# Neighbourhood attention: the products with the values of three query tiles issued in one stretch

## The chip, the core and the metric

The kernel runs on one core of a Trainium2 chip. Its engines work side by side, each through its own queue of instructions in a fixed order: PE (TensorE, matmuls; PEld is the part of it that loads weights), DVE (VectorE), ACT (ScalarE), POOL (GpSimd) and SP (here it issues transfers). SBUF is the on-chip working memory of 128 partitions; PSUM, in eight banks, is where PE writes its results. The metric is the device time of one execution in microseconds (us); less is better. All numbers in this part come from the runs and from one profiled execution of the kernel before.

## The reference

Two layers of a diffusion backbone are computed on 1024 latent tokens (a grid of 16 rows by 64 columns) and 128 context tokens, with a model width of 1024. The first layer has mLSTM heads and grouped-query attention; the change does not touch it. The second layer is neighbourhood attention with 16 heads of width 64: each latent token attends to a window of 8 rows by 16 columns around it and to all 128 context keys, in one softmax. Cut to what matters:

```
s_loc = q_r . k_win * scale + bias              # the window's keys
s_ctx = q_r . kc * scale                        # the 128 context keys
p = softmax(concat([s_loc, s_ctx]))
o = p_loc . v_win + p_ctx . vc
y = (o * silu(z)) @ w_out
```

The last products of `p` with the values `v` and `vc` are what the change moves.

## The kernel before

The kernel is written in a framework that traces the Python code, then orders each engine's instructions by a list scheduler with a model of their times, and inserts the waits. So the order on PE is not the order of the code: while one piece waits for its input, the scheduler puts ready work of another piece ahead of it. A block under `manual_schedule` for an engine keeps its own order there, as one piece.

The second layer (the phase named "na", function `run`, L1383 to L1422) handles the 16 heads as eight pairs, `p` = 0 to 7. For a pair, `na_proj` computes queries, keys, values and the gate from the layer's input. These projections are products in three parts (L328 to L330, and L343 to L345 with the operands swapped), because each number is split into a high and a low part. `na_pair` (L1172) then walks over the queries: eight tiles of 128 latent tokens and one tile of context tokens, in three groups `c` of three tiles. A tile of 128 tokens covers all 16 grid rows of eight neighbouring columns, so its window lies in at most three tiles of keys; with the context keys these are `nk` = 3 (first and last tile) or 4 blocks of 128 keys. The projections of pair p+1 are traced while pair p's attention is under way, and the scheduler mixes both on PE. The last pair has no successor; pieces of its own projections (`late`) and the first tiles of the output projection (`out`) stand in for it.

`na_unit` (L1195) does one tile for both heads of the pair:

- scores (L1210): two products for each head into a bank `s`;
- softmax for each head: DVE adds the bias and finds the maximum (L1216), ACT takes the exponential and the sum (L1218), DVE the reciprocal (L1219), POOL the scaling (L1220), all in a piece of the ring `sb`;
- turning (L1223, recorded at L106): PE transposes the `nk` blocks of weights into the one bank `tr` (in the last pair, the second head uses `ptr`); ACT and DVE take turns to copy that bank into a piece of the ring `pt` (L101, L103);
- products with values (L1227 to L1231): `nk` blocks, and for each block head 0 and then head 1, accumulate in the bank `o`. A product has 64 output rows; the two heads use the two halves of PE's columns (`tile_position=(0, b)`), so their results land in the two halves of `o`.

The three tiles of a group share a bank `o`, of which there is one. Behind the group, `put_y` (L969) multiplies it by the gate into `y` and sends it to memory for the output projection. The ninth tile (context queries) goes through `ctx_unit` (L1004), whose two products with values stand at L1001. All eight pairs together hold 480 products at L1231 (60 in a pair: 6 + 6 x 8 + 6) and 16 at L1001.

The ring `pt` has four pieces of 512 columns, two in each of two tiles (L1390); a piece is free again when the products that read it are done.

Of the kernel before, what the change touches and what calls it, by code (L numbers as in the profile page):

```python
# [18 lines left out]
P = 128  # L19
# [7 lines left out]
DHB = 64  # L27
# [12 lines left out]
class Kern:  # L40
# [42 lines left out]
    def smg(self, w):  # L83
        return self.sp.tile([P, 4], F32, tag="smg", bufs=16, name=self.name("smg"))[:, :w]

    def ring(self, n, bufs):

        ts = [self.u([P, 2, 512], n=n) for _ in range(bufs // 2)]
        turn = itertools.cycle([t[:, i] for t in ts for i in range(2)])
        return lambda: next(turn)  # L90

    def const(self, shape, n, dt=F32):
# [1079 lines left out]
    def na_pair(self, p, terms, v, gz, vc):  # L1172

        nc, a = self.nc, self.a
        bias = []
        for hh in range(2):
            b = self.u([P, T], n="bias")
            nc.sync.dma_start(b, a["na_bias"][2 * p + hh])
            bias.append(b)
        y = self.ytile()  # L1180
        for c in range(NC):
            po = self.ps("o")
            for t in range(3):
                if t:
                    yield y
                j = 3 * c + t
                o = po[:, t * P : (t + 1) * P]
                if j < 8:
                    self.na_unit(terms, v, vc, bias, j, o, p == 7)
                else:  # L1190
                    self.ctx_unit([terms(hh, 8, 11, 1) for hh in range(2)], [v[:, 8, 0:DHB], v[:, 8, DHB:]], o, self.pt)
            self.put_y(p, slice(c * CW, (c + 1) * CW), po, gz, y)
            yield y

    def na_unit(self, terms, v, vc, bias, j, po, alone):  # L1195

        nc = self.nc
        j0, j1 = max(j - 1, 0), min(j + 1, 7)

        k0 = j0 + j0 // 3 + (j0 % 3 > 0)  # L1200
        at = int(k0 % 4 > 0)
        nk = j1 - j0 + 2
        n = nk * P

        first, step, w = (2, 1, P) if j == 0 else (2, 3, P) if j == 7 else (1, 5, 256) if at else (0, 6, 256)
        grid = lambda t: t.rearrange("p (a k) -> p a k", k=w)
        pts, ss = [], [self.ps("s") for _ in range(2)]
        for hh in range(2):
            for part, (x, y) in enumerate(terms(hh, j, k0, nk)):
                nc.tensor.matmul(ss[hh][:, :n], x, y, start=part == 0, stop=part == 1)  # L1210
        for hh in range(2):
            x = self.sb()[:, :n]
            nm = self.sm(1)
            b = bias[hh]
            b = bass.AP(b.tensor, b.offset + first * P, [list(b.ap[0]), [step * P, n // w], [1, w]])
            nc.vector.tensor_tensor_reduce(grid(x), grid(ss[hh][:, :n]), b, -1.0, -NEG, ALU.add, ALU.min, nm)  # L1216
            r = self.sm(1)
            nc.scalar.activation(x, x, AF.Exp, bias=nm, scale=-1.0, accum_out=r)  # L1218
            nc.vector.reciprocal(r, r)  # L1219
            nc.gpsimd.tensor_scalar(x, x, r, 1.0, ALU.mult, ALU.mult)  # L1220
            tr = self.ps("ptr" if alone and hh else "tr")
            for i in range(nk):
                self.flipped(tr[:, i * P : (i + 1) * P], x[:, i * P : (i + 1) * P])  # L1223
            pt = self.pt()
            self.evac(pt[:, :n], tr[:, :n])
            pts.append(pt)
        for i in range(nk):  # L1227
            for hh in range(2):
                b = hh * DHB
                vs = vc[:, b : b + DHB] if i == at else v[:, j0 + i - (i > at), b : b + DHB]  # L1230
                nc.tensor.matmul(po[b : b + DHB, :], vs, pts[hh][:, i * P : (i + 1) * P], start=i == 0, stop=i == nk - 1, tile_position=(0, b))  # L1231


    def run(self):
        nc, a = self.nc, self.a
# [80 lines left out]
        with self.phase("mlstm", ("e", 3, [P, 4, CW])):  # L1316
            self.ts = [self.decays_load(0, g) for g in range(NC)]
            start = self.mlstm_start(0)
# [3 lines left out]
            for hd in range(HA):  # L1322
# [3 lines left out]
                if hd < HA - 1:  # L1326
                    pr = nxt
                    blocks(hd + 1, evs, (2, 3, 4))
                    start = self.mlstm_start(hd + 1)
# [12 lines left out]
        with self.phase("gqa"):  # L1342
            self.pt = self.ring("pt", 14)
            ahead = (w.append(self.w_out(0, k)) for k in range(KB))
            with self.tc.manual_schedule(engines={mybir.EngineType.PE}):
                last = self.gqa(Q, gz, early, ahead)
        gg = [self.load_gg(0, 0, self.raw())]
        h = []
        with self.phase("out0"):
            new = lambda: self.t("x", 5, [P, D])  # L1350
            ys = [self.load_y(i, last) for i in range(2)]
            for c in range(NC):
# [16 lines left out]
                for i in tiles:  # L1369
# [7 lines left out]
                    o, ss = (new(), self.sm(2)) if c < 2 else os[i % 3]  # L1377
# [5 lines left out]
        with self.phase("na"):  # L1383
            self.klo = [self.t(f"kl{j}", 1, [P, 12, P], F32R) for j in range(2)]
            for hh in range(2):
                nc.gpsimd.memset(self.klo[hh][DHB - hh * DHB : 2 * DHB - hh * DHB].bitcast(F32), 0.0)
            for p in range(8):
                tiles, late = self.na_proj(h, p, first)
                if p == 0:
                    self.sb, self.pt = (self.ring(n, 4) for n in ("sb", "pt"))  # L1390
                unit = self.na_pair(p, *tiles)
                if p < 7:
                    for j, _ in enumerate(unit):
                        if late and j in (1, 4, 7):
                            late.pop(0)()
            w, ys, gg = [], [], []

            def out(i):
                if i in (0, 6):
                    gg.append(self.load_gg(1, i // 6, self.u([P, D], n="gg")))  # L1400
                if i + 1 < NT:
                    ys.append(self.load_y(i + 1, last))
                xt = self.u([P, D], n="x")
                nc.sync.dma_start(xt, self.x1d[i * P : (i + 1) * P, :])
                o, ss = self.u([P, D], n="o"), self.sm(2)
                for n in range(2):
                    self.out_half(ys[i], w, n, o, ss, gg[i // 8])
                self.out_end(o, ss, xt, a["out_ys"][i * P : (i + 1) * P, :] if i < 8 else a["out_yp"], 1 + i // 8)

            for j, last in enumerate(unit):  # L1410
                for f in late[j : j + 1]:
                    f()
                for k in range(3 * j, min(3 * j + 3, KB)):
                    w.append(self.w_out(1, k))
                if j == 0:
                    ys = [self.load_y(0, last, False)]
                if j == 2:
                    self.late_y()
                if j in (4, 6):
                    out(j // 2 - 2)  # L1420
            for i in range(2, NT):
                out(i)  # L1422
# [137 lines left out]
```

## Time and profile before

| | |
|---|---|
| median of 3 runs | 1607.9 us (1607.58 to 1609.25) |
| the profiled execution: its time | 1609.35 us |
| its span, first to last instruction | 1607.5 us |
| PE busy | 1555.3 us, 97% of the span |
| DVE / ACT / POOL busy | 848.7 / 655.7 / 603.4 us |
| mean granted TensorE clock | 0.994 |
| records of products with values at L1231 | 960, from 914.7 to 1532.9 us |

The table is of the page that the profiler's data were condensed to. "Busy" is the time in which an engine had an instruction under way. A matmul's end is modelled, and matmuls overlap: a PE that is busy all the time may still lose time between two of them. What a matmul costs is therefore read from the spacing of starts, not from durations. A product of full fp32 numbers, as the turnings' and the values' are, shows as passes: the 480 products at L1231 are 960 records, two for each.

In rows of a timeline, a row is: start in us, duration in us (of the whole row when several equal instructions are merged), engine, line, operation, output<-inputs, rows*columns of the weights and partitions x elements of what is streamed, count, and in brackets the engine's idle time before it with what ended it.

### The profile page before, as it was taken

What the parts mean: (1) busy time and instruction counts of PE and PEld (TensorE: products, weight loads), DVE (VectorE), ACT (ScalarE), POOL (GpSimd) and SP (SyncE); (2) the same over time, 40 slices, a digit from 0 to 9 for tenths busy, and PEclk for the clock granted to TensorE, in tenths of its full rate; (3) what the DMA queues carried; (4) which work ended last, traced back from release to release, by engine and by line L of the source; (5) the groups of instructions that cost most, each with busy time, mean ns of one, the idle gap of its engine ahead of it and who ended that gap; (6) DMA issues with size and microseconds to landing.
All of it is one profiled execution on the core that took longest, in us unless ns stands there. A gap on an engine that the chain in (4) does not pass through costs nothing.

```text
span 1607.5 us, 27178 instructions
## 1 busy us (share of the span) xinstructions
PE 1555.3 (97%) x10190; PEld 1392.0 (87%) x10190; DVE 848.7 (53%) x2324; ACT 655.7 (41%) x1568; POOL 603.4 (38%) x820
## 2 busy tenths in 40 slices
PE   6999998999999899999999999999999999999998
PEld 4899898999999787777889899989998999878776
DVE  3533897974558666774555433343434343446432
ACT  2622212122245677875444433343434333346321
POOL 2415645554446545663224222332323232334100
PEclk9999999999999999999999999999999999999999
DMA  9103635422310000221332212130303030316332
GB/s 358 50 27 108 229 124 193 160 83 90 113 53 28 16 30 22 69 75 62 126 127 97 63 50 83 34 99 22 99 19 99 23 99 19 95 42 193 99 127 79
DMA packets 73122, 143.81 MB, mean 89 GB/s; under 512 B 15466, under 2 KB 44446, under 8 KB 72990
## 3 DMA queue, kind: packets, MB, share of 16 engines
q1 hardware_dynamic: 68692, 127.05, 23.8%
q10 hardware_dynamic: 4298, 15.02, 2.4%
q8 instruction: 81, 1.33, 0.3%
q14 instruction: 51, 0.42, 0.1%
HBM read 115.47 MB, written 21.86 MB: 85 GB/s over the span
## 4 chain that ended last, share of the span: by engine, by line
PE 85%; DVE 8%; ACT 3%; issue 2%; DMA 1%; POOL 1%; SPq 0%; DVEq 0%; POOLq 0%; ACTq 0%
PE pj L330 12%; PE pj L328 12%; PE pj L329 11%; PE pj L343 7%; PE pj L345 7%; PE pj L344 7%; PE tr L106 5%; PE o L1231 5%; PE s L1210 4%; PE o L910 3%; PE s L870 3%; DVE mj L248 3%; PE ptr L106 2%; PE pj L106 2%; DVE pr L871 1%
## 5 line engine op out<-in xcount | busy, mean ns | idle before, releaser
L328 PE MATMUL pj<-hh,whi 128*128 128x384 f32 x1176 | 402.0, 342 | 1.2 <-ACT qT L101 0.5
L330 PE MATMUL pj<-hh,wlo 128*128 128x384 f32 x1176 | 399.5, 341 | 0.6 <-POOL wlo L115 0.6
L329 PE MATMUL pj<-hl,whi 128*128 128x384 f32 x1176 | 399.8, 340 | 0.0
L328 PEld LDWEIGHTS pj<-hh,whi 128*128 128x128 f32 x1176 | 221.6, 188 | 4.4 <-issue 0.7
L329 PEld LDWEIGHTS pj<-hl,whi 128*128 128x128 f32 x1176 | 221.7, 188 | 2.5 <-issue 0.9
L330 PEld LDWEIGHTS pj<-hh,wlo 128*128 128x128 f32 x1176 | 221.3, 188 | 2.6 <-POOL wlo L115 0.8
L1220 POOL TENSOR_SCALAR sb<-sb,sm 128x512 f32<-128x512 f32 (+1 forms) x128 | 85.8, 672 | 306.5 <-DVE sm L1219 289.7
L115 POOL TENSOR_TENSOR wlo<-raw,whi 128x1024 fp32r<-128x1024 f32 x59 | 143.5, 2433 | 133.8 <-ACT whi L114 79.1
L880 POOL TENSOR_SCALAR pr<-pr,smg 128x384 f32<-128x384 f32 x192 | 114.3, 615 | 83.4 <-DVE smg L878 57.1
L1218 ACT ACTIVATE sb<-sb,sm 128x512 f32<-128x512 f32 (+1 forms) x128 | 89.0, 696 | 90.8 <-DVE sm L1216 87.0
L343 PE MATMUL pj<-whi,hh 128*128 128x256 f32 x432 | 122.7, 284 | 1.0 <-DVE v L1136 0.8
L344 PE MATMUL pj<-wlo,hh 128*128 128x256 f32 x432 | 122.1, 283 | 0.0
L345 PE MATMUL pj<-whi,hl 128*128 128x256 f32 x432 | 122.0, 283 | 0.0
L248 DVE CUSTOM_DVE_ANT_0 mj<-wm,cb 128x512 f32<-128x512 f32 x128 | 114.0, 891 | 3.8 <-DMA wm<-in_w_modT_dram 1.8
L871 DVE CUSTOM_DVE_ANT_0 pr<-s,zero 128x384 f32<-128x384 f32 x192 | 102.3, 553 | 24.1 <-PE s L870 23.1
L343 PE MATMUL pj<-whi,yh 128*128 128x512 f32 x288 | 114.1, 396 | 0.0
L344 PE MATMUL pj<-wlo,yh 128*128 128x512 f32 x288 | 114.0, 396 | 0.0
L345 PE MATMUL pj<-whi,yl 128*128 128x512 f32 x288 | 113.6, 395 | 0.0
L870 PE MATMUL s<-Kst,Q 128*128 128x384 f32 x384 | 105.4, 370 | 4.6 <-DVE smg L871 3.7
L1216 DVE CUSTOM_DVE_ANT_1 sb<-s,bias 128x512 f32<-128x512 f32 (+1 forms) x112 | 74.6, 666 | 52.9 <-PE tr L106 49.7
L114 ACT CAST whi<-raw 128x1024 fp32r<-128x1024 f32 x76 | 79.2, 1044 | 29.3 <-DMA raw<-in_w_out_dram 8.3
L343 PEld LDWEIGHTS pj<-whi,hh 128*128 128x128 f32 x432 | 81.4, 188 | 2.9 <-DVE v L1136 1.2
(344 smaller groups left out, 3035.1 us busy)
## 6 DMA issues: line engine op xcount, KB each, us to landing
wm<-in_w_modT_dram SPq DMA_DIRECT2D x32, 512.0 KB, 4.4
raw<-in_w_c_dram SPq DMA_DIRECT2D x25, 512.0 KB, 3.5
raw<-in_w_ab_dram SPq DMA_DIRECT2D x24, 512.0 KB, 4.4
e<-rbd ACTq DMA_DIRECT2D x12, 768.0 KB, 6.1
bias<-in_na_bias_dram SPq DMA_DIRECT2D x16, 576.0 KB, 4.1
wm<-in_w_mod_dram SPq DMA_DIRECT2D x16, 512.0 KB, 6.9
raw<-in_w_out_dram SPq DMA_DIRECT2D x16, 512.0 KB, 3.7
y<-yd SPq DMA_DIRECT2D x18, 448.0 KB, 3.5
```

The costliest lines, as they stand in the source:

```text
L106: self.nc.tensor.transpose(out, in_, self.ident)
L115: (eng_lo or nc.gpsimd).tensor_tensor(lo, src, hi.bitcast(F32), ALU.subtract)
L248: nc.vector.tensor_tensor_reduce(junk, w[:, b, :], cb[:, r, :], 1.0, 0.0, ALU.mult, ALU.add, mp[:, hf, q // 4, 2 * (q % 4) + b, r : r + 1])
L328: nc.tensor.matmul(ps[:, :CW], a, hh, start=k == 0, stop=False)
L329: nc.tensor.matmul(ps[:, :CW], a, hl, start=False, stop=False)
L330: nc.tensor.matmul(ps[:, :CW], b, hh, start=False, stop=k == KB - 1)
L343: nc.tensor.matmul(ps[:, :width], hh, a, start=k == 0, stop=False)
L344: nc.tensor.matmul(ps[:, :width], hh, b, start=False, stop=False)
L345: nc.tensor.matmul(ps[:, :width], hl, a, start=False, stop=k == KB - 1)
L870: nc.tensor.matmul(s[:, :CW], x, y, start=part == 0, stop=part == 1)
L871: nc.vector.tensor_tensor_reduce(pr[:, c, :], s[:, :CW], zero, -1.0, -NEG, ALU.add, ALU.min, m3[:, c : c + 1])
L880: nc.gpsimd.tensor_scalar(pr[:, c, :], pr[:, c, :], r, 1.0, ALU.mult, ALU.mult)
```

## The change

`na_unit` no longer issues the products with values. It returns a function `values` that will, and `na_pair` collects these for the tiles of a group and calls them together behind the group's last tile, in a block that keeps its order on PE. The tiles are taken from the last to the first; inside a tile, head 1 goes ahead of head 0. Since the turned weights of three tiles now have to be kept, the ring `pt` gets seven pieces instead of four: the three new ones are tiles of the phase's own pool (one of two pieces, one of one).

```
-    def ring(self, n, bufs):
+    def ring(self, n, bufs, more=()):
-        ts = [self.u([P, 2, 512], n=n) for _ in range(bufs // 2)]
-        turn = itertools.cycle([t[:, i] for t in ts for i in range(2)])
+        ts = [self.u([P, 2, 512], n=n) for _ in range(bufs // 2)] + list(more)
+        turn = itertools.cycle([t[:, i] for t in ts for i in range(t.shape[1])])
...
             po = self.ps("o")
+            last = []
             for t in range(3):
...
-                    self.na_unit(terms, v, vc, bias, j, o, p == 7)
+                    last.append(self.na_unit(terms, v, vc, bias, j, o, p == 7))
...
+            with self.tc.manual_schedule(engines={mybir.EngineType.PE}):
+                for f in last[::-1]:
+                    f()
             self.put_y(p, slice(c * CW, (c + 1) * CW), po, gz, y)
...
-        for i in range(nk):
-            for hh in range(2):
-                b = hh * DHB
...
+        def values():
+            for i in range(nk):
+                for hh in (1, 0):
+                    b = hh * DHB
...
+        return values
...
-                    self.sb, self.pt = (self.ring(n, 4) for n in ("sb", "pt"))
+                    self.sb, self.pt = self.ring("sb", 4), self.ring("pt", 4, [self.t(f"pt{j}", 1, [P, 2 - j, 512]) for j in range(2)])
```

No instruction is added or taken away on any engine. What moves on PE is seen best in the first group of the first pair. Before, on PE (`s` scores, `tr` turned weights of a tile's head, `o<-pt` products with values, where `vc` are the context's values and `v` the latent tokens'; the number behind a name tells buffers apart):

```order
L106 MATMUL tr_9800<-cc,sb_9778 128x128 x3
L1210 MATMUL s_9860<-k_1670_9381,q_9379 128x512
L1210 MATMUL s_9860<-kl_1662_9369,q_9379 128x512
L1231 MATMUL o_9787<-pt_9780,vc_9373 64x128
L1210 MATMUL s_9861<-k_1671_9382,q_9380 128x512
L1210 MATMUL s_9861<-kl_1663_9370,q_9380 128x512
L106 MATMUL tr_9811<-cc,sb_9778 128x128 x3
L106 MATMUL ptr_9773<-cc,kp_9383 128x128
L1210 MATMUL s_9901<-k_1670_9381,q_9379 128x512
L1210 MATMUL s_9901<-kl_1662_9369,q_9379 128x512
L1231 MATMUL o_9787<-pt_9780,vc_9373 64x128
L1231 MATMUL o_9787<-pt_9780,v_9378 64x128 x4
```

One product of head 0, ready as soon as that head is turned, stands alone between scores; the tile's other five follow once head 1 is turned. With the change the products of this group, on PE:

```order
L1215 MATMUL s_10026<-k_1670_9381,q_9379 128x512
L1215 MATMUL s_10026<-kl_1662_9369,q_9379 128x512
L1238 MATMUL o_9789<-pt_1706_9780,v_9378 64x128 x2
L1238 MATMUL o_9789<-pt_1706_9780,vc_9373 64x128 x2
L1238 MATMUL o_9789<-pt_1706_9780,v_9378 64x128 x4
L1238 MATMUL o_9789<-pt_9783,vc_9373 64x128 x2
L1238 MATMUL o_9789<-pt_9783,v_9378 64x128 x6
L1238 MATMUL o_9789<-pt_9782,vc_9373 64x128 x2
L1238 MATMUL o_9789<-pt_9782,v_9378 64x128 x4
L106 MATMUL tr_9918<-cc,sb_9779 128x128 x4
```

All 22 products of three tiles stand in a row, two heads by turns, the third tile's first. Counted over all of the second layer, with the context tile's pairs of L1001: before, 133 unbroken runs of such products (61 of one product, 8 of two, 15 of five, 1 of six, 46 of seven, 2 of eight); with the change 24 runs (in each pair one of 22, one of 24, one of 16, of which two are the context tile's).

The other place is in pair 6, fourth and fifth tile, where no projection is at hand that could stand between the pieces. Before, on PE:

```order
L106 MATMUL tr_14548<-cc,sb_9779 128x128 x4
L106 MATMUL tr_14560<-cc,sb_9779 128x128 x4
L1231 MATMUL o_14535<-pt_9781,v_13208 64x128
L1210 MATMUL s_14654<-k_2389_14204,q_14202 128x512
L1210 MATMUL s_14654<-kl_1663_9370,q_14202 128x512
L1210 MATMUL s_14691<-k_2388_14203,q_14201 128x384
L1210 MATMUL s_14691<-kl_1662_9369,q_14201 128x384
L1231 MATMUL o_14535<-pt_9781,v_13208 64x128
L1231 MATMUL o_14535<-pt_9781,vc_14103 64x128 x2
L1231 MATMUL o_14535<-pt_9781,v_13208 64x128 x4
L106 MATMUL tr_14586<-cc,sb_9778 128x128 x4
L106 MATMUL tr_14598<-cc,sb_9778 128x128 x4
```

With the change, the same part between two stretches of products, on PE:

```order
L106 MATMUL tr_14607<-cc,sb_9779 128x128 x4
L106 MATMUL tr_14619<-cc,sb_9779 128x128 x4
L1215 MATMUL s_14716<-k_2391_14260,q_14258 128x512
L1215 MATMUL s_14716<-kl_1663_9370,q_14258 128x512
L1215 MATMUL s_14745<-k_2390_14259,q_14257 128x384
L1215 MATMUL s_14745<-kl_1662_9369,q_14257 128x384
L106 MATMUL tr_14637<-cc,sb_9778 128x128 x4
L106 MATMUL tr_14649<-cc,sb_9778 128x128 x4
```

The products that stood between one tile's turnings and the next's are gone from there; only scores are left between them.

More of the change, by code (lines that the diff above doesn't have):

```diff
@@ L1226, in na_unit @@
             pts.append(pt)
-        for i in range(nk):
-            for hh in range(2):
-                b = hh * DHB
-                vs = vc[:, b : b + DHB] if i == at else v[:, j0 + i - (i > at), b : b + DHB]
-                nc.tensor.matmul(po[b : b + DHB, :], vs, pts[hh][:, i * P : (i + 1) * P], start=i == 0, stop=i == nk - 1, tile_position=(0, b))
+        def values():
+            for i in range(nk):
+                for hh in (1, 0):
+                    b = hh * DHB
+                    vs = vc[:, b : b + DHB] if i == at else v[:, j0 + i - (i > at), b : b + DHB]
+                    nc.tensor.matmul(po[b : b + DHB, :], vs, pts[hh][:, i * P : (i + 1) * P], start=i == 0, stop=i == nk - 1, tile_position=(0, b))
+        return values
     def run(self):
```

## The prediction

> **What bounds the kernel now.** I read the page first: the shares of the engines, the granted clock and the chain that ended last.
>
> ```profile
> span 1607.5 us, 27178 instructions
> PE 1555.3 (97%) x10190; PEld 1392.0 (87%) x10190; DVE 848.7 (53%) x2324; ACT 655.7 (41%) x1568; POOL 603.4 (38%) x820
> ...
> PEclk9999999999999999999999999999999999999999
> ...
> PE 85%; DVE 8%; ACT 3%; issue 2%; DMA 1%; POOL 1%; SPq 0%; DVEq 0%; POOLq 0%; ACTq 0%
> ```
>
> PE is the bound on average, at full clock in every slice. The share is a mean over stages, so next come the windows of the stage that changes, from just ahead of the first product at L1231 to behind the last, and who makes PE wait there.
>
> ```profile
> core 0: us, PE busy (x) PEld busy (x) DVE busy (x) ACT busy (x) POOL busy (x), PEclk, DMA share, GB/s
> 909.00:1541.00 632.00, 626.46 (x4237) 555.34 (x4236) 260.38 (x707) 250.80 (x569) 183.51 (x205) 1.00 0.23 71
> ```
>
> ```profile
> engine line waited for: us in total, times, longest us
> PE tr L106 <- DVE pt L103: 2.4, 4, 0.9
> PE pj L343 <- DVE v L1136: 0.8, 2, 0.4
> ...
> PE o L1231 <- DVE pt L103: 0.6, 3, 0.2
> ```
>
> PE is busy for 626 of 632 us and waits for another engine in only a handful of places, while DVE and ACT work 41% and 40% of the time. So a microsecond that PE gets back here is a microsecond of the kernel, unless a new wait eats it. The last query is the line itself.
>
> ```profile
> L1231 PEld LDWEIGHTS o<-pt,v x704: 132/137/137, 917.6 to 1532.9; 128*64 128x64 f32 x176
> L1231 PE MATMUL o<-pt,v x704: 272/273/324, 917.6 to 1533.0; 128*64 128x128 f32 x176
> ...
> L1231 PE MATMUL o<-pt,vc x256: 272/273/324, 914.7 to 1532.6; 128*64 128x128 f32 x128
> ...
>   issue: 20.2, 95
> ```
>
> These are 960 passes for 480 products. "issue 20.2 us, 95 times" is time for which no producer is to blame: PE or its loader stood still for about 0.2 us beside these products. That busy time cannot show all of it is seen in the spacing of starts.
>
> **What a run of products costs.** A run of one product, between turnings and a projection:
>
> ```profile
> 1062.63 0.60 PE L106 MATMUL tr<-cc,sb 128*128 128x128 f32 x4
> 1063.16 0.43 PE L1231 MATMUL o<-pt,v 128*64 128x128 f32 x2
> 1063.53 0.44 PE L328 MATMUL pj<-hh,whi 128*128 128x384 f32 x1
> 1063.80 0.34 PE L329 MATMUL pj<-hl,whi 128*128 128x384 f32 x1
> 1063.98 0.34 PE L330 MATMUL pj<-hh,wlo 128*128 128x384 f32 x1
> ```
>
> ```profile
> L106 PE MATMUL tr<-cc,sb x450: 270/273/329, 913.5 to 1526.8; 128*128 128x128 f32 x150
> ```
>
> Four turnings last 0.60, the last of them 0.27 (the median of the second row), so their starts are 0.11 apart and PE would be free at 1062.63 + 0.44 = 1063.07. The product starts at 1063.16: 0.09 lost. The projection starts 0.37 later, where two passes of 0.11 need 0.22: 0.15 lost. The next projection follows after 0.27 instead of 0.18 (1063.80 to 1063.98): 0.10 lost, with rounding. Together 0.34 us for entering and leaving the form with 64 columns.
>
> A run of seven, between a score and turnings:
>
> ```profile
> 1067.65 0.34 PE L330 MATMUL pj<-hh,wlo 128*128 128x384 f32 x1
> 1067.83 0.34 PE L1210 MATMUL s<-kl,q 128*128 128x384 f32 x1
> 1068.10 0.32 PE L1231 MATMUL o<-pt,v 128*64 128x128 f32 x1
> 1068.10 0.32 PE L1231 MATMUL o<-pt,vc 128*64 128x128 f32 x1
> 1068.26 0.27 PE L1231 MATMUL o<-pt,v 128*64 128x128 f32 x1
> 1068.26 0.38 PE L1231 MATMUL o<-pt,vc 128*64 128x128 f32 x2
> 1068.37 0.27 PE L1231 MATMUL o<-pt,v 128*64 128x128 f32 x1
> 1068.47 0.27 PE L1231 MATMUL o<-pt,vc 128*64 128x128 f32 x1
> 1068.48 0.70 PE L1231 MATMUL o<-pt,v 128*64 128x128 f32 x7
> 1069.11 0.55 PE L106 MATMUL tr<-cc,sb 128*128 128x128 f32 x3
> ```
>
> Two products, one of each head, start together (1068.10 twice, 1068.26 twice) and advance by one pass each 0.11 us. Two heads therefore cost a slot of 0.22 us together, and a product without a partner costs a slot alone: seven products are four slots, 0.88. Entering costs 0.09 (1067.83 + 0.18 to 1068.10). From 1068.10 to the turnings are 1.01, 0.13 more than the slots; three turnings last 0.55 instead of 0.49, another 0.06. Together 0.28; I use 0.29.
>
> **The change part by part.**
>
> Fewer runs. The order has 133 runs before and 24 with the change. Behind 61 of the 133, the runs of one product, stands mostly a score or projection (0.34 each, 20.7); behind the other 72 mostly turnings (0.29 each, 20.9); sum 41.6. The 24 left cost 24 x 0.29 = 7.0. Removed: 34.6 us. By the dearer and cheaper price alone, 109 runs are 37.1 or 31.6.
>
> Full pairs. Slots before: 61 + 8 + 15 x 3 + 3 + 46 x 4 + 2 x 4 = 309. With the change every product has a partner: 496 / 2 = 248. Removed: 61 x 0.22 = 13.4 us. I see no reason for a gain beyond this, since 0.11 for a pass is also the spacing of turnings, which have no partner.
>
> Together -48.0 us of PE, in a stage where PE is the path.
>
> The turning's one bank. The two heads of a tile are turned through the same bank, so the second has to wait until the first is copied:
>
> ```profile
> 1425.16 0.66 PE L106 MATMUL tr<-cc,sb 128*128 128x128 f32 x4
> ...
> 1425.86 0.69 DVE L103 COPY pt<-tr 128x512 f32<-128x512 f32 x1 [3.89 <-PE tr L106]
> ...
> 1426.70 0.63 PE L106 MATMUL tr<-cc,sb 128*128 128x128 f32 x4 [0.40 <-DVE pt L103]
> ```
>
> From start to start are 1.54; less four turnings (0.44) and the 0.06 behind a run, PE needs 1.04 us of other work between two turnings if it isn't to stand. Going through the order with the spacings above, before falls short in 5 places by 4.0 us (the trace shows 2.4 of it as idle; the modelled ends hide the rest), with the change in 11 places by 6.6: products that stood between are gone, most of them in pair 6, the second place shown. Cost +2.6; bounds 0, if the scheduler's gaps fall elsewhere, and 6.6.
>
> The wait at the head. The stretch starts with the head turned last, and everything on PE stands behind it: the next tile's turnings and the projections. From the last turning of a group to the stretch the order has 3.0 to 4.2 us of other work on PE in pairs 0 to 5 (1.28 in the second group of pairs 3 and 5), against the 1.04 needed. Only in pair 6 is it less: 0.9 and 0.7. Cost +0.5; bounds 0 and 24 x 1.04 = 25, a full copy at each stretch. I take the low end, as the cover is visible in the order and the trace has 0.6 us of this wait for 133 runs.
>
> Pair 6 from its fourth tile on: without projections, PE may wait for the softmax itself. The trace shows 0.40 us at a time there; nothing excludes a copy's time, 1.04, for each of four tiles. Bounds 0 and 4.2; I take +1.5, nearer the row.
>
> The ring, seven pieces. Six are held until the stretch, so only one head of the next tile could be turned ahead; the order puts the next turning right behind the stretch anyway. Cost 0 while the stretch is on time. What DVE, ACT and POOL do stays the same in number and kind; DVE and ACT have their 40%.
>
> SP's queue. The transfers of `y` stay behind the group's last product:
>
> ```profile
> SPq L973 <- DVE y L971: 134.2, 17, 25.1
> ```
>
> SP already stands 134 us for `y` with weight loads behind it, and PE's waits above name no load. A `y` some 3 us later costs 0; bounds 0 and 3 us once per pair, 24. Nothing moves ahead of 909 us, and the last 60 us of projections are the same.
>
> Sum: -34.6 - 13.4 + 2.6 + 0.5 + 1.5 = -43.4 us. The profiled execution's own time is 1609.35 (span 1607.5 and 1.85 around it), so it would be 1565.9; the median of the runs is 1.45 lower, which gives 1564.5.
>
> **The rivals.**
>
> Cover runs out. PE ceases to be the path where projections are short, in the second half of pair 6 and in pair 7, and the softmax chain sets the pace: the 6.0 us that each pair would get of the 48.0 are lost for 1.5 pairs, 9 us: 1574. For: the waits of the trace for copies lie there. Against: DVE had been idle for 3.89 us ahead of the copy shown above, which is in pair 6.
>
> Heads wait. Copies come one copy late at each stretch: +25, 1589. For: ACT casts weights between copies:
>
> ```profile
> L114 ACT CAST whi<-raw 128x1024 fp32r<-128x1024 f32 x76 | 79.2, 1044 | 29.3 <-DMA raw<-in_w_out_dram 8.3
> ```
>
> Against: it takes two such casts ahead of a copy to use up 3 us of cover.
>
> Slower: the same wait, but long. A head that waits stops turnings, so copies and the next softmax start later, and the next stretch is late as well. It turns the sign at 43.4 / 24 = 1.8 us for each stretch; with 2.5 the time is 1625. Cover plus wait would then be 5 us for a copy that takes 0.7. Unlikely.
>
> The change doesn't do what it says: the heads don't run side by side in a long stretch. Then 496 slots stand against 309: +187 x 0.22 = +41.1, less 34.6, and 4.6 of waits, +11.1 us: 1619. Against: in the rows of the run of seven, every slot is shared. [...]
>
> **How the numbers follow.** Forecast 0.76; cover runs out 0.12; heads wait 0.07; slower by long waits 0.03; no pairing 0.02. A measurement of this kernel can tell 0.2%, about 3.2 us, from no change; of the heads' case 0.01 may end there. Faster 0.94, same 0.01, slower 0.05. The range goes from no new wait with the trace's 2.4 of turning waits gone and the dearer price for runs (1607.9 - 37.1 - 13.4 - 2.4 = 1555) to beyond the cover case, 1580; left out are the heads' case and the slower ones.
>
> **What would show it.** In the changed profile: 24 runs of products, in each of which starts come in twos, 0.11 apart; a run of 24 is 2.64 and some 0.29 long; the stage from the first score to the last product shorter by 40 to 48; waits of turnings for copies near 5 us in all and those of products under 2. The forecast is wrong if PE shows waits at the stretches' heads above 10 us in sum, if passes in a stretch are further apart than 0.11, or if PE's idle time in pairs 0 to 5 grows by more than 5 us.

## The result and the profile after

The changed kernel takes 1569.9 us (median of 4 runs, 1568.59 to 1571.3), the kernel before 1608.5 beside it; the ratio is 0.976, 95% interval 0.975 to 0.977: 38.5 us faster, where 43.4 were forecast. The page of the profiled execution (its time 1570.01 us):

```profile
span 1568.2 us, 27109 instructions
PE 1512.9 (96%) x10190; PEld 1385.1 (88%) x10190; DVE 847.2 (54%) x2324; ACT 655.0 (42%) x1568; POOL 603.6 (38%) x820
...
PE 84%; DVE 9%; ACT 3%; issue 2%; POOL 1%; DMA 1%; SPq 0%; DVEq 0%; POOLq 0%; ACTq 0%
```

PE's busy time fell by 42.4 us, that of DVE, ACT and POOL by 1.5 at most: the same work, less of PE. The stage's window, and who makes PE wait in it:

```profile
909.00:1501.00 592.00, 583.45 (x4232) 547.46 (x4231) 258.40 (x704) 248.95 (x567) 184.07 (x205) 0.99 0.25 76
```

```profile
PE tr L106 <- DVE pt L103: 3.4, 5, 0.9
PE s L983 <- DVE sm L1221: 1.7, 2, 1.3
PE s L1215 <- DVE sm L1224: 1.0, 1, 1.0
PE s L1215 <- DVE sm L1221: 0.8, 3, 0.3
PE pj L343 <- DVE v L1136: 0.6, 2, 0.4
```

PE now idles for 8.5 us of the stage instead of 5.5, more of it in front of scores that wait for the softmax. Over the stage the clock column is 0.99 instead of 1.00; all of that lies in pair 6 (below). The products' line, from its own view:

```profile
  issue: 2.1, 8
```

The time with no producer to blame beside the products was 20.2 us in 95 places. A stretch of 24 in the second pair, from PE's timeline:

```profile
1046.48 0.34 PE L330 MATMUL pj<-hh,wlo 128*128 128x384 f32 x1
1046.74 0.44 PE L1238 MATMUL o<-pt,v 128*64 128x128 f32 x4
1047.01 0.39 PE L1238 MATMUL o<-pt,vc 128*64 128x128 f32 x4
1047.23 0.61 PE L1238 MATMUL o<-pt,v 128*64 128x128 f32 x8
1047.67 0.39 PE L1238 MATMUL o<-pt,vc 128*64 128x128 f32 x4
1047.89 1.04 PE L1238 MATMUL o<-pt,v 128*64 128x128 f32 x16
1048.76 0.39 PE L1238 MATMUL o<-pt,vc 128*64 128x128 f32 x4
1048.98 0.61 PE L1238 MATMUL o<-pt,v 128*64 128x128 f32 x8
1049.52 0.66 PE L106 MATMUL tr<-cc,sb 128*128 128x128 f32 x4
```

The 48 passes from 1046.74 to 1049.52 take 2.78 us. They go two at a time, one on each half of the columns, so 24 x 0.11 = 2.64 us of it are passes, and 0.14 is the cost of the run's entry and exit; with 0.15 more in the spacings of its neighbours, this is the one run's 0.29. It is what the prediction said a run of 24 would look like. One stretch does not:

```profile
1046.81 2.77 PE o L1238 x48
...
1406.47 4.40 PE o L1238 x48
```

These two rows of the chain in order of time are the same 24 products, in the second group of pair 1 and of pair 6. The second is at half clock (below).

To compare kernels I split the stage, from 909 us to the start of the last gate multiplication (DVE, `y<-o,gz`), in three. "Products" are slots x 0.218 and, for each run, 0.295 where turnings follow and 0.344 else (the median spacings of before over 72 and 61 runs), so this column is counted and priced, not measured; "other work" is every other record on PE times its usual spacing (0.109 for a turning, which is one record where a product is two; 0.118, 0.175 and 0.231 for 256, 384 and 512 columns, about 0.06 for the few others of 128); "rest" is what remains: waits, and time lost to a slower clock. At 909 us the kernels aren't equally far: their first scores stand between 905.6 and 907.7 us. The column of other work takes that up.

| kernel | runs | slots | stage | products | other work | rest | of it pair 0 | pairs 1-5 | pair 6 | pair 7 |
|---|---|---|---|---|---|---|---|---|---|---|
| before | 133 | 309 | 630.2 | 109.5 | 509.4 | 11.3 | 2.1 | 3.5 | 5.4 | 0.3 |
| changed | 24 | 248 | 591.4 | 61.2 | 509.5 | 20.6 | 4.6 | 5.0 | 10.4 | 0.7 |
| by tile (e2) | 72 | 248 | 600.7 | 75.5 | 509.3 | 15.9 | 3.0 | 5.2 | 7.3 | 0.4 |
| first tile first (e4) | 57 | 248 | 593.3 | 72.5 | 510.4 | 10.3 | 3.0 | 2.6 | 4.4 | 0.3 |
| the same in pairs 0 and 6 (e8) | 32 | 248 | 586.8 | 63.9 | 509.1 | 13.7 | 3.0 | 4.9 | 5.1 | 0.7 |

At these prices the products gave back 48.3 us. The rest grew by 9.3, of which 5.0 are in pair 6, 2.5 in pair 0 and 1.5 in pairs 1 to 5. That is the whole difference, 48.3 - 9.3 = 39.0 against a stage that is 38.8 shorter. The prices can be held against the traces: what all spacings into, through and out of the runs take beyond their slots is 43.7 us before, 9.2 with the change (1.6 of it the stretch at half clock), 22.1 in e2, 19.7 in e4 and 10.6 in e8.

### The profile page after: what moved, and what is told of

The parts are those of the page before. It is cut to its first block, busy times and chain, and to the rows that moved or that the text cites. A ratio compares the mean times of both kernels' runs of the same rounds, so it can differ in the third digit from the quotient of the medians.

```text
span 1568.2 us, 27109 instructions
## 1 busy us (share of the span) xinstructions
PE 1512.9 (96%) x10190; PEld 1385.1 (88%) x10190; DVE 847.2 (54%) x2324; ACT 655.0 (42%) x1568; POOL 603.6 (38%) x820
## 4 chain that ended last, share of the span: by engine, by line
PE 84%; DVE 9%; ACT 3%; issue 2%; POOL 1%; DMA 1%; SPq 0%; DVEq 0%; POOLq 0%; ACTq 0%
PE pj L328 12%; PE pj L330 12%; PE pj L329 12%; PE pj L343 7%; PE pj L344 7%; PE pj L345 7%; PE tr L106 5%; PE o L1238 4%; PE o L910 3%; PE s L1215 3%; PE s L870 3%; DVE mj L248 3%; PE ptr L106 2%; PE pj L106 2%; DVE pr L871 1%
```

## The experiments

The theory: PE is the path, each run of products costs 0.29 to 0.34 us of PE and each slot 0.22, and what is not gained is waits where PE has no other work. The rivals: the ring of seven does it; the pairing of heads is no part of it; waits move rather than go.

**The ring alone (e1).** The kernel before, with the new `ring` and

```
...
-                    self.sb, self.pt = (self.ring(n, 4) for n in ("sb", "pt"))
+                    self.sb, self.pt = self.ring("sb", 4), self.ring("pt", 4, [self.t(f"pt{j}", 1, [P, 2 - j, 512]) for j in range(2)])
```

> The kernel before with the ring of seven pieces alone; its PE order still has 133 runs in 309 slots. If runs and slots are the cause (0.29 to 0.34 us for each run, 0.22 for each slot): no change, ratio to before 0.999 to 1.001. If the gain comes from the deeper ring, which lets turned weights wait: most of the 38.5 us, near 1570 to 1580.

Measured: 1608.1 us, ratio to before 1.000 (0.999 to 1.001). The ring is needed to hold three tiles, but gives nothing by itself; that rival is out.

**One stretch for each tile (e2).**

```
-                    last.append(self.na_unit(terms, v, vc, bias, j, o, p == 7))
+                    f = self.na_unit(terms, v, vc, bias, j, o, p == 7)
+                    with self.tc.manual_schedule(engines={mybir.EngineType.PE}):
+                        f()
...
-            with self.tc.manual_schedule(engines={mybir.EngineType.PE}):
-                for f in last[::-1]:
-                    f()
...
```

Against the changed kernel, with the ring of four.

> The products of each tile in one stretch, both heads by turns, with the ring of four pieces: 72 runs in 248 slots. Runs and slots: 61 runs fewer than before (61 x 0.34 = 20.7) and 61 slots fewer (13.4) give 34 us off before, less new waits of 0 to 3, so 1574 to 1578; in pair 6 products stand between turnings again, so PE's idle time there is near that of before. If the deeper ring is what matters: 1590 or more. If the long stretch is what costs the waits in pair 6: PE's clock doesn't fall there.

Measured: 1578.7 us, ratio 0.9815 (0.980 to 0.983). Three quarters of the gain come without a deeper ring and without joining tiles. The time is 0.7 above the range expected. Runs and slots are 34.0 at the table's prices (109.5 - 75.5), as counted ahead; by the spacings in its trace the runs cost 22.1 us, 21.6 less than before, and the 61 slots are another 13.3. The rest grew by 4.6, where 0 to 3 were expected. The clock stays at 1.00 in pair 6. Its "issue" row lies between the other two:

```profile
  issue: 9.9, 38
```

**The two heads apart (e3).**

```
-            for i in range(nk):
-                for hh in (1, 0):
+            for hh in (1, 0):
+                for i in range(nk):
```

> The changed kernel, but in each tile all products of head 1 first, then all of head 0: the same 24 runs, neighbours mostly on the same half of PE's columns. If two heads run at once only as neighbours: of a tile's four blocks only the neighbours at the seams pair up, 19, 17 and 12 slots instead of 12, 11 and 8 in a pair, 136 x 0.22 = +30 us, near 1600; without any pairing at the seams 240 x 0.22 = +53, near 1622. If the pairing is no part of the gain: 1570.

Measured: 1582.6 us in one run, 12.6 above the change, none of the three. The stretches of 24 in the chain, and the head of one in PE's timeline:

```profile
1049.69 3.48 PE o L1238 x48
```

```profile
1049.62 0.43 PE L1238 MATMUL o<-pt,v 128*64 128x128 f32 x2
1049.89 0.38 PE L1238 MATMUL o<-pt,vc 128*64 128x128 f32 x2
1050.11 0.49 PE L1238 MATMUL o<-pt,v 128*64 128x128 f32 x5
1050.38 0.27 PE L1238 MATMUL o<-pt,vc 128*64 128x128 f32 x1
```

Four passes of head 1 start alone up to 1050.00, a fifth at 1050.11, and together with it head 0 begins, though its first product is queued behind four of head 1. So here the halves did not need neighbours in the queue: the second half started, 0.49 us after the first, when two of the four products ahead of its own had gone and the third began. Each stretch of 24 takes 3.48 instead of 2.77, 0.71 more, each of 22 and of 16 0.60 and 0.49 more by the same spacings, 14.4 us for eight of each; less some 1.6 for the change's stretch at half clock, as the clock stays full here (the stretch in pair 6, from 1417.61 us, takes 3.48 too), that is near the 12.6 measured. One after the other, 48 passes would have been 5.2 (48 x 0.109, an estimate). Alternating heads is worth having, but less than I priced it.

**First tile first (e4).**

```
-                for f in last[::-1]:
+                for f in last:
```

> The changed kernel with the tiles of a group taken from the first to the last. Its PE order has 57 runs in 248 slots, since other work now fits in ahead of the tile turned last. Runs and slots: 33 more runs than the change, 33 x 0.30 = +10, near 1580, less up to 3 of waits that such work covers. If the number of runs doesn't matter once the heads are paired: 1570 or less.

Measured: 1570.8 us, ratio 0.9767 (0.9751 to 0.9784), the change's time and not near 1580; by the time alone, the number of runs would not matter. The trace says otherwise: by its own spacings the 57 runs cost 19.7 us, the change's 24 cost 9.2 (11.3 us more at the table's prices), but the rest falls by 10.3. With the first tile first, a tile's products can go as soon as they are ready, and the scheduler sets them into the holes that the last tile leaves. Last tile first makes the stretch one piece and takes away this filler. The two orders trade one for the other.

**More cover for pair 6 (e5): its gate projection held back.**

```
-        if 0 < p < 7 and p % 2 == 0:
+        if 0 < p < 6 and p % 2 == 0:
...
-            if p % 2:
+            if p % 2 or p == 6:
```

> The changed kernel with the gate projection of pair 6 held back (as in the odd pairs) and given out in three parts between its tiles, so that PE has projections there. Before these runs, the changed kernel has 10.4 us in pair 6 that are neither work nor runs (before 5.4), with the granted clock down to 0.5 around 1405 us. If missing cover is the cause: those fall to 2 to 5, the clock stays at full, 1562 to 1566. If the softmax chain of DVE and ACT is the limit there: no change, 1569 to 1571.

Measured: 1570.9 us, ratio 0.9771 (0.9756 to 0.9786): nothing gained, the time that was expected if the softmax chain is the limit there. The trace is of an execution of 1574.05 us. In it the rest in pair 6 fell to 7.4, but that of pairs 1 to 5 rose to 11.3, with pair 5 at 7.5. PE's work is the same in all, so work held back for one hole opens another. The clock is at half from 1335.1 to 1341.9 us, in pair 5, and again in pair 6:

```profile
1400.00:1405.00 5.00, 3.94 (x24) 2.66 (x23) 3.02 (x10) 3.25 (x8) 1.57 (x3) 1.00 0.00 0
1405.00:1410.00 5.00, 3.65 (x14) 2.71 (x14) 4.00 (x13) 3.62 (x9) 2.96 (x4) 0.68 0.00 2
```

**Pair 6 by tile (e6).**

```
-                    last.append(self.na_unit(terms, v, vc, bias, j, o, p == 7))
+                    f = self.na_unit(terms, v, vc, bias, j, o, p == 7)
+                    if p == 6:
+                        with self.tc.manual_schedule(engines={mybir.EngineType.PE}):
+                            f()
+                    else:
+                        last.append(f)
```

> The changed kernel with pair 6's products in one stretch for each tile, so that they stand between turnings there again: 30 runs in 248 slots. Six more runs cost 6 x 0.3 = 1.8; PE's time without work in pair 6 goes from 10.4 to about the 7.3 of the kernel in which all pairs are by tile, without the fall of the clock: 1568 to 1570. If the waits in pair 6 have nothing to do with the long stretch: 1571 to 1572.

Measured: 1569.9 us, ratio 0.9762 (0.9747 to 0.9777). The rest in pair 6 went from 10.4 to 8.6, and six more runs cost the 1.8 us that this gave; the clock still fell, to 0.75 between 1405 and 1410 us, which I had not expected.

**A second bank for turning in pair 6 (e7).**

```
-                    last.append(self.na_unit(terms, v, vc, bias, j, o, p == 7))
+                    last.append(self.na_unit(terms, v, vc, bias, j, o, p >= 6))
```

> The changed kernel with a second bank for turning the second head in pair 6 as in pair 7. The three waits of turnings for copies in pair 6 (2.2 us) go. If they start the idle stretch: PE's time without work there falls by 3 to 5, the clock stays, 1565 to 1567. If the next wait (scores for the softmax, 2.3 us there) takes their place: 1569 to 1571.

Measured: 1567.6 us (1565.5 to 1572.7), ratio 0.9743 (0.9727 to 0.9759). It looks some 2 us better, but the intervals overlap. The trace is of the longest execution, 1572.67 us; it is long because its first score comes at 910.1 us instead of 907.4, and from there to the last gate multiplication it takes as long as the change (592.8 and 593.0 us). In it pair 6's rest is 4.3 and pair 7's 6.7, together what they were: the hole moved. The shorter executions have no trace.

**First tile first in pairs 0 and 6 (e8), and again beside the change (e11, e12).**

```
-                for f in last[::-1]:
+                for f in last if p in (0, 6) else last[::-1]:
```

> The changed kernel, with the first tile first in pairs 0 and 6 alone, where PE waited, and the last tile first elsewhere: 32 runs in 248 slots. With the first tile first everywhere the time without work or runs was 3.0 in pair 0 and 4.4 in pair 6 (4.6 and 10.4 in the changed kernel), but 57 runs took 11.3 us more. If long runs where cover is plenty and short ones where it isn't add up: -7.6 + 8 x 0.3 = -5, near 1565. If the waits only move to the next pair: 1569 to 1571.

Measured: 1566.2 us, ratio 0.9739 (0.9724 to 0.9753), close to the 1565 expected; its row is in the table. The interval still touched the change's, so both were measured once more, side by side.

> The changed kernel as it is, beside the next one on the same chip: 1569 to 1571.

> The kernel with the first tile first in pairs 0 and 6 alone, beside the changed kernel. If what its trace showed (2.7 us more for runs, 6.9 less of time without work) is no accident of one execution: 3 to 5 us under the changed kernel, 1565 to 1567, with intervals that don't meet. If it is: within 1 us of it.

Measured: the change 1570.2 us, ratio 0.9757 (0.9743 to 0.9770), the other 1564.5, ratio 0.9728 (0.9715 to 0.9741); the intervals just don't meet. So this order is faster than the kernel before and the change, but not by all of the 5.7 us: in the two traces 2.1 of them lie ahead of the first score (907.9 and 905.8 us). From there to the last gate multiplication it takes 588.8 us in both of its traces and the change 593.0 and 592.9, so 4.1 us are the order's. Windows through pair 6 in its second trace, with no fall of the clock:

```profile
1395.00:1400.00 5.00, 4.22 (x39) 3.19 (x40) 3.21 (x12) 3.33 (x10) 2.09 (x3) 1.00 0.00 0
1400.00:1405.00 5.00, 4.01 (x43) 3.00 (x41) 3.63 (x13) 3.74 (x11) 3.29 (x3) 1.00 0.14 31
1405.00:1410.00 5.00, 5.00 (x31) 4.81 (x32) 1.22 (x3) 1.75 (x4) 3.07 (x4) 1.00 0.94 289
```

**Head 0 first (e9).**

```
-                for hh in (1, 0):
+                for hh in range(2):
```

> The changed kernel with head 0 ahead of head 1 in each block. Its PE order has 39 runs in 263 slots: in 15 of the 24 groups the very first product, whose head was turned earlier, is issued alone ahead of the rest. Runs and slots: 15 x 0.34 + 15 x 0.22 = +8.4, near 1578, less what such a product covers of a wait (nothing or 1 to 2). If the order of the heads doesn't matter: 1570.

Measured: 1575.7 us, ratio 0.9801 (0.9785 to 0.9817). At the table's prices the products grew by 8.4, as expected, and the rest fell by 2.7. Head 1 is turned last, so a stretch that starts with it has nothing that could go ahead of it; this is what the order of the heads is for.

**Both measures in pair 6 (e10).** First tile first in pairs 0 and 6, and `p >= 6` for the bank.

> First tile first in pairs 0 and 6 (1566.2 alone) and a second bank for turning in pair 6 (1567.6 alone): 33 runs in 249 slots. If both take away different waits of pair 6: 1562 to 1564. If the hole that PE has there only moves to pair 7, as with the bank alone: 1565 to 1568.

Measured: 1565.9 us, ratio 0.9738 (0.9723 to 0.9753): not told apart from e8. Pair 6 has 2.0 of rest and pair 7 4.2; the bank moves the hole on.

## Why the prediction was right, and where it was off

**PE is the path, and spacings price it: right.** Fewer runs were put at -34.6 us. By the spacings of all runs in the two traces they cost 43.7 us before and 9.2 after (1.6 of it the slow stretch): -34.5. Full pairs: 61 slots as counted, -13.4 forecast, -13.3 at 0.218 for a slot. Together -47.8 against -48.0. The cause has experiments behind it: the ring alone gives nothing (e1), and kernels with 72, 57 and 32 runs pay 0.31 to 0.35 us for each by their own spacings (e2, e4, e8).

**The waits were mis-sized.** The terms +2.6, +0.5 and +1.5 for copies, stretch heads and the softmax chain add up to 4.6; the rest grew by 9.3. By the prediction's own account most of the 4.6 stood in pair 6, and there the rest did grow by 5.0. What failed is that it put the other pairs at nothing: pair 0, whose first groups have hardly any projections either, grew by 2.5, pairs 1 to 5 by 1.5. That pair 6 comes out near is partly luck, for 1.6 to 3.4 of its 5.0 are a clock that no term of the sum has (below). The waits on PE's list there went from 3.3 to 4.5 us, with those for copies at 2.4 before and 2.2 after; the new waits for copies are in pair 0 (1.3). Over the stage they are 3.4 us, where near 5 was forecast. Stretch heads cost nothing that the list of waits shows. PE's idle time by the profile grew by 3.0 us; with the clock that leaves some 3 to 5 of the 9.3 that no view names, probably short waits that the modelled ends hide; that stays open. So the stage from the first score to the last product is 38.5 us shorter, under the 40 to 48 that the prediction named as a sign; the others held or nearly so, but passes are further than 0.11 apart in the one stretch at half clock (20 of them, two at a time, take from 1406.40 to 1408.59 us: 0.22 apart). What stood behind pair 6 is this part of the timeline of PE and DVE:

```profile
1399.24 0.63 PE L106 MATMUL tr<-cc,sb 128*128 128x128 f32 x4 [0.88 <-DVE pt L103]
...
1400.77 0.33 PE L983 MATMUL s<-k,q 128*128 128x128 f32 x1 [0.40 <-DVE sm L1221]
...
1401.23 0.63 PE L106 MATMUL tr<-cc,sb 128*128 128x128 f32 x4
1401.61 1.01 DVE L354 TENSOR_TENSOR gz<-th,pj 128x384 f32<-128x384 f32 x2
1402.53 0.55 DVE L1221 CUSTOM_DVE_ANT_1 sb<-s,bias 128x384 f32<-128x384 f32 x1
...
1403.15 0.48 PE L983 MATMUL s<-k,q 128*128 128x128 f32 x1 [1.29 <-DVE sm L1221]
```

Turnings wait for copies, scores for the softmax to free a bank, and DVE puts two gate multiplications (1.01 us) ahead of that softmax, so PE stands for 1.29 us. Before, the products of single tiles filled such gaps: PE was busy 3.7 to 4.3 of every 5 us there.

**The clock was not in the sum.** The prediction read "full clock in every slice" from digits that mean 90% or more, a mean of 0.994; in the stage that was so (1.00). Windows of 5 us in pair 6, before and then after (the last columns but two are the granted clock):

```profile
1426.00:1431.00 5.00, 4.29 (x30) 2.47 (x28) 2.70 (x9) 2.10 (x5) 1.39 (x2) 1.00 0.01 2
1431.00:1436.00 5.00, 3.74 (x28) 2.47 (x28) 2.65 (x8) 2.00 (x5) 1.39 (x2) 1.00 0.11 39
1436.00:1441.00 5.00, 3.94 (x30) 2.76 (x30) 4.22 (x13) 2.39 (x6) 1.39 (x2) 1.00 0.01 3
```

```profile
1395.00:1400.00 5.00, 3.09 (x17) 2.10 (x18) 3.37 (x10) 2.21 (x6) 1.39 (x2) 1.00 0.11 39
1400.00:1405.00 5.00, 3.23 (x15) 2.16 (x15) 3.67 (x12) 3.67 (x9) 2.12 (x4) 0.80 0.01 2
1405.00:1410.00 5.00, 5.00 (x40) 4.56 (x42) 1.60 (x7) 2.55 (x9) 2.84 (x2) 0.52 0.64 198
```

PE is granted half its clock from 1402.96 to 1409.79 us, and the stretch that falls into this takes 4.40 us instead of 2.77. The price is 1.6 us at least (that stretch) and 3.4 at most (half of 6.83, part of which PE would have waited anyway). If the hole set the fall off, which no run shows by itself, it cost more than the waits that the page lists.

**The rivals.** "Cover runs out" is what happened, at about half of its 9 us and inside the forecast's own range; it began earlier in pair 6 than I put it, lay in pair 0 too, and was nearly nothing in pair 7 (+0.4). "Heads wait" did not happen. The pairing rival was wrong in its price: even with the heads apart it would have been 14, not 41 us (e3), since there products on different halves of the columns ran together without being neighbours (3.48 us for a stretch of 24). The slow case through long waits had nothing for it.

**What the order does.** I took "last tile first" as given. It and "head 1 first" are what keeps a stretch in one piece (e4, e9). That one piece is worth 10 us of runs and costs 10 us of filler was shown only by trying the other order.

## What to carry to other kernels

Read what a change of form costs PE from the spacing of starts around it, multiply by the number of unbroken runs in the order: that way the gain of joining runs came out here to a microsecond (34.6 put, 34.5 by the spacings). Then look at where the joined pieces had been filling holes: where PE has other work, join; where it hasn't, leave them apart, as in the kernel that joins all but two pairs. Held-back work and a second bank did not close the hole in their traces, they moved it.

## What the runs showed of the hardware

Entering and leaving products on half of the columns cost PE 0.29 to 0.34 us for each run in these traces, 0.34 for one of a single product and 0.29 for one of 24. In e3 the two halves advanced each on its own: with the heads apart, the second half started 0.49 us after the first (1049.62 and 1050.11 us), not after its four products (0.9, an estimate of eight passes at 0.109).

In pair 6 of the change PE had no idle time over 1.3 us, and its clock was 0.50 from 1402.96 to 1409.79 us. What sets such a fall off is not shown. In the last window of 5 us ahead of it, from 1395 us, PE was busy for 3.09 us. Pair 6 alone by tile (e6), where the clock fell, and all pairs by tile (e2), where it didn't, each from its emptiest 5 us in pair 6 on:

```profile
1400.00:1405.00 5.00, 3.54 (x32) 2.40 (x30) 3.81 (x11) 2.00 (x5) 1.06 (x3) 1.00 0.01 2
1405.00:1410.00 5.00, 3.92 (x26) 3.12 (x26) 2.93 (x11) 4.28 (x12) 3.94 (x4) 0.75 0.31 96
1410.00:1415.00 5.00, 5.00 (x31) 4.68 (x28) 1.25 (x2) 1.95 (x2) 1.72 (x3) 0.91 0.71 236
```

```profile
1405.00:1410.00 5.00, 3.47 (x29) 2.29 (x28) 2.63 (x10) 2.38 (x8) 1.39 (x2) 1.00 0.00 0
1410.00:1415.00 5.00, 3.73 (x31) 2.90 (x32) 3.88 (x14) 3.35 (x8) 2.56 (x4) 1.00 0.02 3
1415.00:1420.00 5.00, 5.00 (x41) 4.42 (x40) 1.90 (x5) 2.32 (x5) 2.48 (x3) 1.00 0.67 203
```

Busy time, with its modelled ends, doesn't part them: 3.54 of 5 us in e6 ahead of the window with the fall, and 3.47 and then 3.73 in e2 with none.
